# A two-layer decoder trunk in exact fp32: the MLA mask and maximum as one VectorE operation, values behind the scores of two groups, words for transposes, and small loads issued later

## The chip, the core and the metric

The kernel runs on one core of a Trainium2 chip. The metric is the time of one execution on the device in microseconds (us). The core has TensorE (PE: matrix products from SBUF into the accumulation memory PSUM; loading the stationary operand is shown apart as PEld), VectorE (DVE), ScalarE (ACT), GpSimd (POOL) and SyncE (SP, here the queue that issues the weight loads).

## The reference

Two residual layers over 256 positions of width 2048, all in float32. The even layer runs 32 state-space heads (convolution, silu, chunked scan) and 16 heads of latent attention (MLA) from one input projection, and projects both outputs together; the odd layer is stick-breaking attention; each is followed by a SwiGLU feed-forward part of 5632 hidden units.

```python
def reference(x, ...):
    for layer in range(2):
        h = rms_norm(x, mix_norm[layer])
        mix = ssd_mla_mixer(h, ...) if layer % 2 == 0 else stick_breaking_mixer(h, ...)
        x = x + mix
        x = x + swiglu_ffn(rms_norm(x, ffn_norm[layer]), w_gate[layer], w_up[layer], w_down[layer])
    return rms_norm(x, final_norm)

def mla_mixer(...):   # for each block of 128 query rows, queries q0 to q1
    s = (q_nope @ k_nope.T + q_pe @ k_pe.T) * 192 ** -0.5    # keys 0 to q1
    mask = jnp.arange(q1)[None, :] <= jnp.arange(q0, q1)[:, None]
    p = jax.nn.softmax(jnp.where(mask, s, -jnp.inf), axis=-1)
    out = p @ v
```

## The kernel before

**Exactness.** A weight tile of 128x2048 arrives as `w`. ScalarE casts it to fp32r (the form in which TensorE takes a 32-bit word in one pass) as the high part `wh` (line 346), and VectorE subtracts to get the low part in place of `w` (line 352). Activations are split in the same way. Each product of tiles is three matmuls: high by high, low by high, high by low (lines 460, 462 and 463 in `project`, 508 and 510 in `project_T`, and line 905 in `pair`, which does the large products by a scheme of seven block products M1 to M7, with sums and differences of weight tiles in `wsum` slots, line 852). A transpose is a matmul with an identity; `transpose` (lines 356 to 359) takes an fp32r source with the fp32r identity at line 357, and any other with the fp32 identity at line 359. A "twin" is a piece of SBUF that has two names: `raw` in fp32 and `words` in fp32r. The same holds for the residual blocks `xres` and `xwords`.

**Order.** TensorE's order is the order of the program. Small work runs as generator tasks: `spawn` starts one, each `yield n` puts it to sleep for n steps, and each `tick` (one step of a projection, mostly) wakes at most two tasks that are due. The other engines' orders come from a scheduler by priorities. Weight tiles have rising numbers `wprio`, tasks marked `URGENT` come ahead of them; the loads of weights are issued by SyncE in order of `wprio`.

**Start.** `constants` issues x and the first norm's gains on SyncE, and calls `small_loads` at once: ten loads on GpSimd's queue (four norms' gains, convolution weights and bias, the three head parameters `hp`, `rope`). `constant_tiles` makes the identities (`ident`, `ident_r`, and a bf16 `identb`), triangles and the bf16 mask tile `cmask`. The loaded rows are transposed on TensorE by `vectors` (line 314) at the end of the first input projection.

**Even layer.** `even` runs six projections for the convolution, two for the latent q and kv, four for the gate z, the output projection's state-space half, then the MLA groups and the output's MLA half. `conv` writes a block's channels into `s2` buffers and ends with a silu (line 1504); `ssd_group` transposes them (line 1562) four at a time.

**MLA.** `mla_group` handles four heads: it projects the rope half of q, then q, k and v, and spawns four `mla_head` tasks, four steps apart, which run during the next group's projections. A head makes scores in one PSUM tile of 128x384 (queries 0 to 127 against 128 keys, queries 128 to 255 against 256 keys): lines 1649 and 1650 multiply, and line 1651 adds the mask as a bf16 matmul of `identb` by `cmask`. VectorE takes two maxima (line 1656) and scales them (1657), ScalarE exponentiates with the sum (1659), VectorE divides. Seven steps later TensorE transposes p (line 1667, three transposes), ScalarE copies it (1669), and four steps later come the two products with v. Scores, transposes and products with v share a ring of four PSUM buffers, `tr`.

**Norms.** `norm_block` transposes a residual block of 512 columns in fours (through `transpose_split`). The blocks between the output projections and the feed-forward parts are spawned by `norm_next`; their blocks 2 and 3 read `xres`.

Of the kernel before, what the change touches and what calls it, by code (L numbers as in the profile page):

```python
# [15 lines left out]
P = 128  # L16
# [31 lines left out]
class Trunk:  # L48
# [84 lines left out]
    def weight_slots(self):  # L133
# [7 lines left out]
        for k in range(n):  # L141
# [27 lines left out]
        self.spare = [at(f"spare{q}", [P, 512], q) for q in range(8)]  # L169

    def wsum(self):
# [50 lines left out]
    def constants(self):  # L222
# [10 lines left out]
        for j in range(1, 4):  # L233
            with self.priority(self.wprio + 1000 * j - 500):
                nc.sync.dma_start(self.xres[j],
                                  i["x"][0, :, j * 512:(j + 1) * 512].rearrange("(t p) d -> p t d", p=P))
        with self.priority(self.wprio + 3500):
            self.small_loads(rows_a, rows_b)
        with self.priority(self.wprio + 6500):
# [11 lines left out]
    def small_loads(self, rows_a, rows_b):  # L251
        nc, i = self.nc, self.i
        c = lambda shape, name, dt=F32: self.cp.tile(shape, dt, name=name)
        for r0, r1, name in ((0, 32, "ffn_norm"), (32, 48, "ssd_norm"), (48, 52, "q_norm"), (52, 56, "kv_norm")):
            nc.gpsimd.dma_start(rows_a[r0:r1], i[name].rearrange("l (k p) -> (l k) p", p=P))
        nc.gpsimd.dma_start(rows_b[0:96], i["conv_w"].rearrange("e j (k p) -> (e j k) p", p=P))
        nc.gpsimd.dma_start(rows_b[96:120], i["conv_b"].rearrange("e (k p) -> (e k) p", p=P))
        self.hp = c([P, 3, 32], "hp")
        for r, name in enumerate(("dt_bias", "a_log", "d_skip")):
            nc.gpsimd.dma_start(self.hp[:, r, :], i[name][0:1, :].partition_broadcast(P))  # L260
        self.rope = c([P, 2, 2, 32], "rope")
        nc.gpsimd.dma_start(self.rope, i["rope"].rearrange("(t p) c d -> p t c d", p=P))


    def constant_tiles(self, rows_m, rows_a, rows_b):
# [24 lines left out]
        self.ones = self.ones_r.bitcast(F32)  # L290
        zero = self.s2([P])
        nc.gpsimd.memset(zero, 0.0)
# [997 lines left out]
    def even(self, st):  # L1290
        nc, i = self.nc, self.i
        win = i["w_in"][0]
        xT = self.pairs(st["xT"], True)
        xdt = [[self.spare[2 * n + t] for t in range(2)] for n in range(4)]
        y = [[self.s2([512]) for _ in range(2)] for _ in range(4)]
# [67 lines left out]
        oT = self.operand()  # L1363
        for g in range(4):
            self.mla_group(g, self.pairs(cT[:1]), self.pairs(cT[1:]), oT)
        st = self.norm_begin()
# [117 lines left out]
    def conv(self, n, res):  # L1484

        nc = self.nc
        for k2 in range(2):
            yield (8 if n == 4 else 2) if k2 == 0 else 1
            pt = self.tr([2, S])
            for k in range(2):  # L1490
                for t in range(2):
                    c = (2 * k2 + k) * P
                    self.transpose(pt[:, k, t * P:(t + 1) * P], self.twins[t].words[:, c:c + P])
            o = self.s2([2, S])
            res.append(o)
            for k in range(2):
# [33 lines left out]
    def ssd_group(self, g, conv, cconv, cb, xdt, y):  # L1530
# [28 lines left out]
        for t in range(2):  # L1559
            pt = self.tr([512])  # L1560
            for k in range(4):
                nc.tensor.transpose(pt[:, k * P:(k + 1) * P], xT[k // 2][:, k % 2, t * P:(t + 1) * P], self.ident)
# [23 lines left out]

    def mla_group(self, g, cq, ckv, oT):
# [3 lines left out]
        h0 = 4 * g  # L1591

        def heads(wd, c0, n):
            def view(w, k0, k1):
                for k in range(k0, k1):
                    yield (w[:, k - k0, :4 * n].rearrange("p (h c) -> p h c", c=n),
                           wd[:, k, h0:h0 + 4, c0:c0 + n])
            return view

        qp = self.evac_rope(self.project(cq, heads(wuq, 128, 64), 4, 256), self.twins[g % 2])  # L1600
        q = self.project_T(cq, heads(wuq, 0, 128))
        k = self.project_T(ckv, heads(wkv, 0, 128))
        v = self.evac(self.project(ckv, heads(wkv, 128, 128), 4))
        o, left = self.out_tiles(g), [0, 1, 2, 3]

        def done(h):
            left.remove(h)
            if g < 2 and not left:
                with self.priority(10000000):
                    self.operand_ready(oT, g, o, 1)  # L1610
        tasks = [self.spawn(self.mla_head(h, qp, q, k, v, g, o, 2 + 4 * h, done), self.URGENT) for h in range(4)]
        oT["xT"].append((self.spawn(self.wait_all(tasks)), o))

# [25 lines left out]
    def mla_head(self, h, qp, q, k, v, g, o, wait, done):  # L1639
# [7 lines left out]
        for q0, q1, c0, ks in ((0, P, 0, P), (P, S, P, S)):  # L1647
            dst = sc[:, c0:c0 + ks]
            nc.tensor.matmul(dst, qT[:, q0:q1], kT[:, 0:ks], start=True, stop=False)  # L1649
            nc.tensor.matmul(dst, qpT[:, q0:q1], self.kpeT[:, h % 2, 0:ks], start=False, stop=False)  # L1650
            nc.tensor.matmul(dst[:, ks - P:ks], self.identb, self.cmask, start=False, stop=True)
        mx, sm = self.small([P, 2], "mx"), self.small([P, 2], "sm")
        p = self.s2([3 * P])
        regs = (slice(0, P), slice(P, 3 * P))
        for t in range(2):
            nc.vector.tensor_reduce(mx[:, t:t + 1], sc[:, regs[t]], AX.X, ALU.max)
# [71 lines left out]
```

## Time and profile before

| | us |
|---|---|
| three runs | 2367.43, 2367.01, 2366.98 |
| median | 2367.01 |
| the profiled execution, its own time | 2367.28 |
| its span in the profile | 2365.2 |
| granted clock of TensorE, as a share | 0.998 |
| MLA heads on TensorE, start of the first scores to start of the last product with v | 422.6 to 553.8 |

The span is the time from the first to the last recorded instruction; 2.1 us lie around it. The profile's 40 slices have TensorE at nine tenths or more in all but the last. A row of a timeline tells the start, the duration, the engine, the line, the operation as output<-inputs, the sizes, the type and the number of joined records. TensorE's matmuls overlap, so that what one costs is read from the start of one to the start of the next. A row of the groups tells the total busy time, the mean in ns, and idle time just before with what ended it.

### The profile page before, as it was taken

To read this page: it belongs to the slowest core of one execution; us is meant where nothing else is said; L and a number is where in the kernel's file an instruction comes from. 1 tells how busy PE (TensorE), PEld (TensorE's weight loads), DVE (VectorE), ACT (ScalarE), POOL (GpSimd) and SP (SyncE) were. 2 spreads that over 40 slices of the span, in tenths; PEclk is the share of its full clock that TensorE was granted. 3 is DMA by queue.
4 is the path that set the end of the run, shared out by engine and by line. 5 is a ranking of instruction groups with operands and counts; after the bars stand their busy time and mean duration, and the time that the engine had idled before them with its cause. 6 is when DMAs were issued, how large, how long until landed. Compare 5 with 4: busy or idle time off the path is not lost.

```text
span 2365.2 us, 28220 instructions
## 1 busy us (share of the span) xinstructions
PE 2349.3 (99%) x11082; PEld 1953.9 (83%) x11082; DVE 2001.6 (85%) x1657; ACT 1467.2 (62%) x1486; POOL 215.7 (9%) x273
## 2 busy tenths in 40 slices
PE   9999999999999999999999999999999999999998
PEld 7888888988888888888888888888888888888886
DVE  6776587589998889989887898889997988989895
ACT  6655565566665655566665786776664656556664
POOL 1342001110000000000000020110000000000011
PEclk9999999999999999999999999999999999999999
DMA  7665556445666777777776555557667777767773
GB/s 273 204 194 179 184 196 188 135 142 195 231 203 207 225 217 215 223 219 221 218 241 207 203 182 176 185 175 242 226 203 213 216 228 221 217 214 228 216 253 110
DMA packets 271428, 486.33 MB, mean 206 GB/s; under 512 B 22268, under 2 KB 47488, under 8 KB 271296
## 3 DMA queue, kind: packets, MB, share of 16 engines
q1 hardware_dynamic: 255200, 445.95, 57.3%
q0 software_dynamic: 15232, 37.01, 6.5%
q8 instruction: 87, 1.43, 0.2%
q10 hardware_dynamic: 864, 1.57, 0.2%
q14 instruction: 45, 0.37, 0.0%
HBM read 459.24 MB, written 25.20 MB: 205 GB/s over the span
## 4 chain that ended last, share of the span: by engine, by line
PE 95%; DVE 2%; ACT 2%; issue 1%; DMA 0%; SPq 0%; ACTq 0%; DVEq 0%
PE acc L905 54%; PE acc L460 11%; PE acc L463 11%; PE acc L462 11%; PE tr L357 1%; PE acc L643 1%; PE acc L508 1%; ACT wh L346 1%; PE at L1578 1%; PE acc L510 0%; DVE wsum L852 0%; DVE wsum L352 0%; DVE w L352 0%; PE at L1649 0%; DMA xres<-in_x_dram 0%
## 5 line engine op out<-in xcount | busy, mean ns | idle before, releaser
L352 DVE TENSOR_TENSOR w<-w,wh 128x2048 fp32r<-128x2048 f32 (+2 forms) x399 | 893.4, 2246 | 174.8 <-ACT wh L346 168.4
L905 PE MATMUL acc<-wh,s 128*128 128x512 f32 x3896 | 985.4, 391 | 1.6 <-ACT s L926 1.2
L346 ACT CAST wh<-w 128x2048 fp32r<-128x2048 f32 (+2 forms) x399 | 744.5, 1874 | 322.9 <-PE acc L463 135.3
L905 PEld LDWEIGHTS acc<-wh,s 128*128 128x128 f32 x3896 | 725.5, 188 | 151.0 <-ACT s L926 1.7
L460 PE MATMUL acc<-wh,s 128*128 128x512 f32 (+1 forms) x1168 | 463.4, 397 | 0.1
L463 PE MATMUL acc<-wh,s 128*128 128x512 f32 (+1 forms) x1168 | 452.4, 387 | 0.2 <-DVE s L381 0.2
L462 PE MATMUL acc<-w,s 128*128 128x512 f32 (+1 forms) x1104 | 426.7, 387 | 0.0
L905 PE MATMUL acc<-w,s 128*128 128x512 f32 x1312 | 355.6, 389 | 0.2 <-DVE w L352 0.2
L905 PEld LDWEIGHTS acc<-w,s 128*128 128x128 f32 x1312 | 246.2, 188 | 52.1 <-DVE w L352 0.6
L463 PEld LDWEIGHTS acc<-wh,s 128*128 128x128 f32 x1168 | 219.3, 188 | 46.1 <-DVE s L381 0.6
L460 PEld LDWEIGHTS acc<-wh,s 128*128 128x128 f32 x1168 | 219.4, 188 | 43.6 <-issue 1.7
L462 PEld LDWEIGHTS acc<-w,s 128*128 128x128 f32 x1104 | 207.7, 188 | 40.0 <-issue 1.4
L352 DVE TENSOR_TENSOR wsum<-wsum,wh 128x2048 fp32r<-128x2048 f32 (+1 forms) x103 | 222.1, 2156 | 3.4 <-ACT wh L346 3.3
L346 ACT CAST wh<-wsum 128x2048 fp32r<-128x2048 f32 (+1 forms) x103 | 185.8, 1804 | 57.5 <-PE acc L905 38.4
L1067 POOL DMA_DIRECT2D saved<-s x64 | 55.9, 996 | 1107.0 <-ACT s L1066 1105.8
L346 ACT CAST wh<-lent 128x2048 fp32r<-128x2048 f32 (+1 forms) x62 | 114.6, 1858 | 62.4 <-DMA lent<-in_w_gate_dram 26.0
L352 DVE TENSOR_TENSOR lent<-lent,wh 128x2048 fp32r<-128x2048 f32 (+1 forms) x62 | 137.1, 2217 | 11.6 <-ACT wh L346 11.1
L852 DVE TENSOR_TENSOR wsum<-w,wsum 128x2048 f32<-128x2048 f32 (+1 forms) x54 | 106.7, 1976 | 19.2 <-PE acc L905 16.6
L905 PE MATMUL acc<-wsum,s 128*128 128x512 f32 x380 | 104.6, 390 | 1.4 <-DVE wsum L352 1.4
L905 PEld LDWEIGHTS acc<-wsum,s 128*128 128x128 f32 x380 | 71.2, 188 | 17.1 <-DVE wsum L352 2.2
L926 ACT COPY s<-acc 128x512 f32<-128x512 f32 x88 | 51.6, 588 | 39.1 <-PE acc L905 39.1
L852 DVE TENSOR_TENSOR wsum<-w,w 128x2048 f32<-128x2048 f32 (+1 forms) x36 | 72.6, 2017 | 1.7 <-DMA w<-in_w_qkv_dram 1.7
(280 smaller groups left out, 1966.8 us busy)
## 6 DMA issues: line engine op xcount, KB each, us to landing
w<-in_w_down_dram SPq DMA_DIRECT2D x80, 1024.0 KB, 4.9
w<-in_w_gate_dram SPq DMA_DIRECT2D x76, 1024.0 KB, 5.1
w<-in_w_up_dram SPq DMA_DIRECT2D x76, 1024.0 KB, 5.1
w<-in_w_qkv_dram SPq DMA_DIRECT2D x48, 1024.0 KB, 5.0
w<-in_w_in_dram SPq DMA_DIRECT2D x45, 1024.0 KB, 5.1
w<-in_w_out_even_dram SPq DMA_DIRECT2D x32, 1024.0 KB, 4.9
saved<-s POOLq DMA_DIRECT2D x64, 256.0 KB, 7.3
w<-in_w_out_odd_dram SPq DMA_DIRECT2D x16, 1024.0 KB, 5.0
```

The source lines that it names most:

```text
L346: cast = nc.scalar.copy(hi, src).ins
L352: return nc.vector.tensor_tensor(lo, src, hi.bitcast(F32), op=ALU.subtract).ins
L357: self.nc.tensor.transpose(out.bitcast(F32R), src, self.ident_r)
L460: nc.tensor.matmul(ps[t], hi[:, ts], wh, start=k == 0, stop=False)
L462: slot.used(nc.tensor.matmul(ps[t], hi[:, ts], wl, start=False, stop=False), self.clock)
L463: nc.tensor.matmul(ps[t], lo[:, ts], wh, start=False, stop=k == nk - 1)
L508: nc.tensor.matmul(ps[:, h % 2], wh[:, hs], x, start=k == n == 0, stop=False)
L643: m = nc.tensor.matmul(ps[b], x, y, start=b not in started, stop=stop, skip_group_check=True)
L852: ins = self.nc.vector.tensor_tensor(half(o, so), half(p, sp), half(q, sq), op=ALU.subtract).ins
L905: m = nc.tensor.matmul(ps[b], x, y, start=b not in started, stop=stop, skip_group_check=True)
L926: copied = nc.scalar.copy(o, ps[b]).ins
L1067: nc.gpsimd.dma_start(self.saved[n][:, t], s, accum_op=ALU.add)
```

## The change

Five edits stand in it.

**1. Mask and maximum.** The two mask matmuls of a head go, and with them `identb` and `cmask`. GpSimd fills a tile `mask` of 128x256 fp32 (zeros on the left, the causal mask on the right) behind the state-space half of the output projection. One VectorE operation a region adds the mask to the scores, multiplies by −scale, writes the result (the wide region in place in PSUM, the narrow one into p), and gives the minimum as the exponential's bias. The exponential's scale becomes −1.

**2. Values later.** `mla` takes the place of `mla_group`: scores of groups 0 and 1 first, then the values of both, then the same for 2 and 3. Heads of the second of a pair are three steps apart, and the first head of a pair waits eight steps, not four, before its products with v.

**3. Words.** Eight leases of 2 KB, each with an fp32 and an fp32r name, lie over the two `wsum` slots. The convolution's outputs for blocks 0 to 3 and p of eleven heads (groups 0 and 1, and three of group 2) stand there, and are transposed as words. So are blocks 2 and 3 of the norms behind the output projections; only the very first block keeps `xres`.

**4. Small loads.** `small_loads` runs as a task eight steps into the first projection, and each load waits for the latest weight cast on ScalarE at that point. On GpSimd the loads stand behind the triangles, `hp` and `rope` first.

**5. Filler.** A constant `more_filler` takes the room of what is gone, in the pool of constants.

```diff
@@ weight_slots
+        first = self.HIGH + self.LOW
+        lease = lambda k, name, dt: nc.alloc_sbuf_tensor_at(
+            f"{name}{k}", [P, 512], dt, offset=base + 8192 * first + 2048 * k).ap()
+        self.leases = [Twin(lease(k, "lease", F32), lease(k, "leasewords", F32R)) for k in range(8)]
...
@@ constants, small_loads, even
-        with self.priority(self.wprio + 3500):
+        def vectors_in():
+            yield 8
             self.small_loads(rows_a, rows_b)
+        def load(dst, src):
+            ins = nc.gpsimd.dma_start(dst, src).ins
+            self.tc.add_manual_dep(ins, self.cast.name, mybir.DependencyInfo(
+                mybir.DependencyClass.Sync, mybir.DependencyReason.DATA), reason="behind the first tiles")
+        self.spawn(self.vectors_in())
@@ constant_tiles
-        self.identb = c([P, P], "identb", BF16)
-        make_identity(nc, self.identb)
...
-        self.cmask = c([P, P], "cmask", BF16)
-        nc.gpsimd.affine_select(self.cmask, zero, [[-1, P]], ALU.is_ge, NEG, base=0, channel_multiplier=1)
+        c([P, P], "more_filler")
@@ norm_block
-        x = (self.xres if rank and rank < 100000 else self.xwords)[j]
+        x = (self.xres if rank == 99600 else self.xwords)[j]
@@ conv
-            o = self.s2([2, S])
-            res.append(o)
+            if n < 4:
+                o, w = (a.rearrange("p (k s) -> p k s", k=2) for a in self.lease(2 * n + k2))
+                res.append(w)
+            else:
+                o = self.s2([2, S])
+                res.append(o)
@@ ssd_group
-                nc.tensor.transpose(pt[:, k * P:(k + 1) * P], xT[k // 2][:, k % 2, t * P:(t + 1) * P], self.ident)
+                self.transpose(pt[:, k * P:(k + 1) * P], xT[k // 2][:, k % 2, t * P:(t + 1) * P])
@@ mla, in place of mla_group
+        for g in (0, 2):
+            scores(g, 4)
+            scores(g + 1, 3)
+            values(g)
+            values(g + 1)
@@ mla_head
-            nc.tensor.matmul(dst, qpT[:, q0:q1], self.kpeT[:, h % 2, 0:ks], start=False, stop=False)
-            nc.tensor.matmul(dst[:, ks - P:ks], self.identb, self.cmask, start=False, stop=True)
+            nc.tensor.matmul(dst, qpT[:, q0:q1], self.kpeT[:, h % 2, 0:ks], start=False, stop=True)
...
+        if g < 2 or g == 2 and h < 3:
+            p, words = (a[:, :3 * P] for a in self.lease(4 * (g > 0) + h))
+        else:
+            p = words = self.s2([3 * P])
...
-        for t in range(2):
-            nc.vector.tensor_reduce(mx[:, t:t + 1], sc[:, regs[t]], AX.X, ALU.max)
-        nc.vector.tensor_scalar(mx, mx, -scale, None, op0=ALU.mult)
-        for t in range(2):
-            nc.scalar.activation(p[:, regs[t]], sc[:, regs[t]], AF.Exp, scale=scale, bias=mx[:, t:t + 1],
+        for t in (1, 0):
+            with self.tc.issue_after(first) if first else nullcontext():
+                first = nc.vector.tensor_tensor_reduce((p, sc)[t][:, regs[t]], sc[:, regs[t]],
+                                                       self.mask[:, P * (1 - t):], -scale, -NEG, ALU.add, ALU.min,
+                                                       mx[t]).ins
+        for t in (1, 0):
+            nc.scalar.activation(p[:, regs[t]], (p, sc)[t][:, regs[t]], AF.Exp, scale=-1.0, bias=mx[t],
                                  accum_out=sm[:, t:t + 1])
...
-            nc.tensor.transpose(pt[:, b * P:(b + 1) * P], p[:, b * P:(b + 1) * P], self.ident)
+            self.transpose(pt[:, b * P:(b + 1) * P], words[:, b * P:(b + 1) * P])
...
-        yield 4
+        yield 8 if h == 0 and g % 2 == 0 else 4
```

TensorE at the first MLA head's scores, before; `at` is the PSUM tile of scores, `acc` that of the projection around it:

```order
L463 MATMUL acc_3280<-wh_67,s_201_1855 128x256
L1649 MATMUL at_3299<-s_303_3205,s_299_3145 128x128
L1650 MATMUL at_3299<-kpeT,s_306_3225 128x128
L1651 LDWEIGHTS identb
L1651 MATMUL at_3299<-cmask,identb 128x128
L1649 MATMUL at_3299<-s_303_3205,s_299_3145 128x256
L1650 MATMUL at_3299<-kpeT,s_306_3225 128x256
L1651 LDWEIGHTS identb
L1651 MATMUL at_3299<-cmask,identb 128x128
L460 MATMUL acc_3279<-wh_67,s_204_1881 128x256
```

The same place of the changed kernel, whose lines 1678 and 1679 are 1649 and 1650 of before:

```order
L474 MATMUL acc_3247<-wh_66,s_192_1853 128x256
L1678 MATMUL at_3266<-s_295_3208,s_291_3148 128x128
L1679 MATMUL at_3266<-kpeT,s_298_3228 128x128
L1678 MATMUL at_3266<-s_295_3208,s_291_3148 128x256
L1679 MATMUL at_3266<-kpeT,s_298_3228 128x256
L471 MATMUL acc_3246<-wh_66,s_195_1879 128x256
```

Two matmuls and their loads of the identity are gone, and the same projection matmul follows.

ScalarE at the end of the second convolution block, before; the two silus are L1504 ACTIVATE, and the casts are of weight tiles:

```order
L1499 ACTIVATE s_141_1178<-tr_1173,vb 128x256
L1553 ACTIVATE s_134_1138<-s_134_1138 128x512
L1504 ACT_TABLE_LOAD
L1504 ACTIVATE s_139_1157<-s_139_1157 128x512
L346 CAST wh_65<-w_76 128x2048
L1504 ACTIVATE s_141_1178<-s_141_1178 128x512
```

And of the changed kernel, where the silu is L1523, the cast L357, and the block stands in leases:

```order
L1518 ACTIVATE lease_112<-tr_1176,vb 128x256
L1572 ACTIVATE s_131_1142<-s_131_1142 128x512
L357 CAST wh_67<-w_74 128x2048
L1591 COPY s_138_1249<-at_1247 128x512
L1523 ACT_TABLE_LOAD
L1523 ACTIVATE lease_110<-lease_110 128x512
L1523 ACTIVATE lease_112<-lease_112 128x512
```

No cast stands between the two silus now; one cast and a copy that stood elsewhere come ahead of both.

VectorE at a head of group 1 in the changed kernel (L1689 is the new operation, which the program lists as two: the operation and the read of its minimum; L363 is a weight split):

```order
L1689 ISA at_3608,mx_357_3614<-at_3608,s_286_3065 128x256
L1689 ISA mx_357_3614 128x1
L363 TENSOR_TENSOR w_79<-w_80,wh_66 128x4x256
L1689 ISA lease_118,mx_356_3613<-at_3608,s_286_3065 128x128
L1689 ISA mx_356_3613 128x1
L1695 RECIPROCAL sm_3615<-sm_3615 128x2
L1697 TENSOR_SCALAR lease_118<-lease_118,sm_3615 128x128
L1697 TENSOR_SCALAR lease_118<-lease_118,sm_3615 128x256
```

A head of group 1 before, where L1656 is a maximum, L1657 the scaling of both, and L352 a weight split:

```order
L352 TENSOR_TENSOR w_79<-w_80,wh_66 128x2048
L1656 TENSOR_REDUCE mx_3618<-at_3611 128x1 x2
L1657 TENSOR_SCALAR mx_3618<-mx_3618 128x2
L352 TENSOR_TENSOR w_77<-w_78,wh_67 128x4x256
L1661 RECIPROCAL sm_3619<-sm_3619 128x2
L1663 TENSOR_SCALAR s_362_3620<-s_362_3620,sm_3619 128x128
L1663 TENSOR_SCALAR s_362_3620<-s_362_3620,sm_3619 128x256
```

The split, which stood behind the two maxima, stands between the two new operations.

More of the change, by code (lines that the diff above doesn't have):

```diff
@@ L169, in weight_slots, with lease @@
         self.spare = [at(f"spare{q}", [P, 512], q) for q in range(8)]
+    def lease(self, k):
+        return self.leases[k].raw, self.leases[k].words
     def wsum(self):
@@ L236, in constants @@
                                   i["x"][0, :, j * 512:(j + 1) * 512].rearrange("(t p) d -> p t d", p=P))
-        with self.priority(self.wprio + 3500):
+        def vectors_in():
+            yield 8
             self.small_loads(rows_a, rows_b)
+        self.vectors_in = vectors_in
         with self.priority(self.wprio + 6500):
@@ L252, in small_loads @@
         nc, i = self.nc, self.i
+        def load(dst, src):
+            ins = nc.gpsimd.dma_start(dst, src).ins
+            self.tc.add_manual_dep(ins, self.cast.name, mybir.DependencyInfo(
+                mybir.DependencyClass.Sync, mybir.DependencyReason.DATA), reason="behind the first tiles")
         c = lambda shape, name, dt=F32: self.cp.tile(shape, dt, name=name)
         for r0, r1, name in ((0, 32, "ffn_norm"), (32, 48, "ssd_norm"), (48, 52, "q_norm"), (52, 56, "kv_norm")):
-            nc.gpsimd.dma_start(rows_a[r0:r1], i[name].rearrange("l (k p) -> (l k) p", p=P))
-        nc.gpsimd.dma_start(rows_b[0:96], i["conv_w"].rearrange("e j (k p) -> (e j k) p", p=P))
-        nc.gpsimd.dma_start(rows_b[96:120], i["conv_b"].rearrange("e (k p) -> (e k) p", p=P))
+            load(rows_a[r0:r1], i[name].rearrange("l (k p) -> (l k) p", p=P))
+        load(rows_b[0:96], i["conv_w"].rearrange("e j (k p) -> (e j k) p", p=P))
+        load(rows_b[96:120], i["conv_b"].rearrange("e (k p) -> (e k) p", p=P))
         self.hp = c([P, 3, 32], "hp")
         for r, name in enumerate(("dt_bias", "a_log", "d_skip")):
-            nc.gpsimd.dma_start(self.hp[:, r, :], i[name][0:1, :].partition_broadcast(P))
+            load(self.hp[:, r, :], i[name][0:1, :].partition_broadcast(P))
         self.rope = c([P, 2, 2, 32], "rope")
-        nc.gpsimd.dma_start(self.rope, i["rope"].rearrange("(t p) c d -> p t c d", p=P))
+        load(self.rope, i["rope"].rearrange("(t p) c d -> p t c d", p=P))
     def constant_tiles(self, rows_m, rows_a, rows_b):
@@ L290, in constant_tiles @@
         self.ones = self.ones_r.bitcast(F32)
-        zero = self.s2([P])
-        nc.gpsimd.memset(zero, 0.0)
-        self.cmask = c([P, P], "cmask", BF16)
-        nc.gpsimd.affine_select(self.cmask, zero, [[-1, P]], ALU.is_ge, NEG, base=0, channel_multiplier=1)
+        c([P, P], "more_filler")
         self.vm, self.va, self.vb = c([P, 32], "vm"), c([P, 56], "va"), c([P, 120], "vb")
@@ L1363, in even @@
         oT = self.operand()
-        for g in range(4):
-            self.mla_group(g, self.pairs(cT[:1]), self.pairs(cT[1:]), oT)
+        self.mask = self.s2([2 * P])
+        nc.gpsimd.memset(self.mask, 0.0)
+        nc.gpsimd.affine_select(self.mask[:, P:], self.mask[:, P:], [[-1, P]], ALU.is_ge, NEG, base=0,
+                                channel_multiplier=1)
+        self.mla(self.pairs(cT[:1]), self.pairs(cT[1:]), oT)
         st = self.norm_begin()
@@ L1585, in ssd_group, with mla @@
         nc.gpsimd.tensor_tensor(y[1], y[1], yo, op=ALU.add)
-    def mla_group(self, g, cq, ckv, oT):
+    def mla(self, cq, ckv, oT):
         nc, i = self.nc, self.i
@@ L1590, in mla_group, with heads @@
         wkv = i["w_ukv"][0].rearrange("(k p) (h c) -> p k h c", p=P, c=256)
-        h0 = 4 * g
-        def heads(wd, c0, n):
+        def heads(wd, g, c0, n):
             def view(w, k0, k1):
@@ L1596, in view, with scores, done, values @@
                     yield (w[:, k - k0, :4 * n].rearrange("p (h c) -> p h c", c=n),
-                           wd[:, k, h0:h0 + 4, c0:c0 + n])
+                           wd[:, k, 4 * g:4 * g + 4, c0:c0 + n])
             return view
[L1600 to L1612, printed above, removed]
+        v = [[] for _ in range(4)]
+        def scores(g, gap):
+            qp = self.evac_rope(self.project(cq, heads(wuq, g, 128, 64), 4, 256), self.twins[g % 2])
+            q = self.project_T(cq, heads(wuq, g, 0, 128))
+            k = self.project_T(ckv, heads(wkv, g, 0, 128))
+            o, left = self.out_tiles(g), [0, 1, 2, 3]
+            def done(h):
+                left.remove(h)
+                if g < 2 and not left:
+                    with self.priority(10000000):
+                        self.operand_ready(oT, g, o, 1)
+            tasks = [self.spawn(self.mla_head(h, qp, q, k, v[g], g, o, 2 + gap * h, done), self.URGENT)
+                     for h in range(4)]
+            oT["xT"].append((self.spawn(self.wait_all(tasks)), o))
+        def values(g):
+            v[g] += self.evac(self.project(ckv, heads(wkv, g, 128, 128), 4))
+        for g in (0, 2):
[3 more added lines that the diff above has]
+            values(g + 1)
     def wait_all(self, tasks):
@@ L1649, in mla_head @@
             nc.tensor.matmul(dst, qT[:, q0:q1], kT[:, 0:ks], start=True, stop=False)
[L1650 to L1653, printed above, removed]
-        regs = (slice(0, P), slice(P, 3 * P))
-        for t in range(2):
-            nc.vector.tensor_reduce(mx[:, t:t + 1], sc[:, regs[t]], AX.X, ALU.max)
-        nc.vector.tensor_scalar(mx, mx, -scale, None, op0=ALU.mult)
-        for t in range(2):
-            nc.scalar.activation(p[:, regs[t]], sc[:, regs[t]], AF.Exp, scale=scale, bias=mx[:, t:t + 1],
+            nc.tensor.matmul(dst, qpT[:, q0:q1], self.kpeT[:, h % 2, 0:ks], start=False, stop=True)
+        mx, sm = [self.small([P, 1], f"mx{t}") for t in range(2)], self.small([P, 2], "sm")
+        if g < 2 or g == 2 and h < 3:
+            p, words = (a[:, :3 * P] for a in self.lease(4 * (g > 0) + h))
+        else:
+            p = words = self.s2([3 * P])
+        regs = (slice(0, P), slice(P, 3 * P))
+        first = None
+        for t in (1, 0):
[5 more added lines that the diff above has]
+            nc.scalar.activation(p[:, regs[t]], (p, sc)[t][:, regs[t]], AF.Exp, scale=-1.0, bias=mx[t],
                                  accum_out=sm[:, t:t + 1])
```

## Prediction

> **What bounds the kernel now.** I read the page's first part, then its chain of work, then TensorE's list of waits, because a kernel with one engine near 100% is changed only by what that engine does and by what it waits for.
>
> ```profile
> PE 2349.3 (99%) x11082; PEld 1953.9 (83%) x11082; DVE 2001.6 (85%) x1657; ACT 1467.2 (62%) x1486; POOL 215.7 (9%) x273
> ...
> PE 95%; DVE 2%; ACT 2%; issue 1%; DMA 0%; SPq 0%; ACTq 0%; DVEq 0%
> ```
>
> ```profile
> PE acc L905 <- DVE wsum L352: 1.4, 2, 0.7
> ...
> PE acc L905 <- ACT s L926: 1.2, 1, 1.2
> PE tr L357 <- DMA xres<-in_x_dram: 0.6, 1, 0.6
> PE at L1518 <- ACT s L1504: 0.6, 1, 0.6
> ```
>
> TensorE works for 2349.3 us of a span of 2365.2, and the chain is 95% TensorE. All its waits in the list together are under 8 us. So I count records that leave TensorE's sequence, records that get shorter, and waits that go or come. VectorE's 2001.6 us matter only in stretches where it is full. The sum is made against the profiled execution, 2367.28 us (its span and 2.1 us around it); the median of the three runs, 2367.01, lies 0.3 below it. About 0.2% of it, 4.7 us, is what a measurement of this kernel tells from no change, so "faster" means below 2362.3.
>
> **The mask leaves TensorE (32 matmuls).** Part of TensorE's own timeline around the first MLA head; the columns are start, duration, engine, line, operation and the number of records joined:
>
> ```profile
> 423.03 0.22 PE L1651 MATMUL at<-cmask,identb 128*128 128x128 bf16 x1
> 423.08 0.65 PE L1649 MATMUL at<-s,s 128*128 128x256 f32 x2
> 423.57 0.59 PE L1650 MATMUL at<-kpeT,s 128*128 128x256 f32 x2
> 424.00 0.22 PE L1651 MATMUL at<-cmask,identb 128*128 128x128 bf16 x1
> 424.03 0.36 PE L460 MATMUL acc<-wh,s 128*128 128x256 f32 x1
> 424.23 0.28 PE L462 MATMUL acc<-w,s 128*128 128x256 f32 x1
> 424.35 0.28 PE L463 MATMUL acc<-wh,s 128*128 128x256 f32 x1
> ```
>
> Durations overlap, so the cost is in the starts. The first mask starts at 423.03 and the next record at 423.08: 0.05 us. That next pair then takes 0.49 to its successor where the equal pair behind it takes 0.43: 0.06 more. The second mask takes 0.03, and the projection matmul behind it 0.20 (424.03 to 424.23) where the next takes 0.12: 0.08. Either way a mask costs 0.11 us, so 32 cost **3.5 us**. Bounds: the mask's own steps alone, 0.03 to 0.05, give 1.3; its recorded duration gives 7.0:
>
> ```profile
> L1651 PE MATMUL at<-cmask,identb 128*128 128x128 bf16 x32 | 7.0, 219 | 0.0
> ```
>
> I take 3.5, as the lengthened neighbours are measured.
>
> **Words for transposes.** Three kinds of transposes read fp32r instead of fp32: 32 of the state-space groups (L1562), 33 of the 48 at L1667, and 32 of the 40 at L359 (blocks 2 and 3 of the norms, in both layers). The two forms stand beside each other in the feed-forward part, each as four transposes followed by four matmuls of 128x512:
>
> ```profile
> 610.01 0.60 PE L359 MATMUL tr<-ident,xres 128*128 128x128 f32 x4
> 610.36 1.17 PE L905 MATMUL acc<-wh,s 128*128 128x512 f32 x4
> 611.38 0.60 PE L359 MATMUL tr<-ident,xres 128*128 128x128 f32 x4
> ```
>
> ```profile
> 664.93 0.46 PE L357 MATMUL tr<-ident_r,twinwords 128*128 128x128 f32 x4
> 665.23 1.16 PE L905 MATMUL acc<-wh,s 128*128 128x512 f32 x4
> 666.22 0.46 PE L357 MATMUL tr<-ident_r,twinwords 128*128 128x128 f32 x4
> ```
>
> From start to start the fp32 period is 1.37 us, the fp32r period 1.29: 0.08 for four transposes. The state-space groups are eight fours: **0.64**. The eleven heads have threes at 0.06: **0.66**. The norms would give another 0.64, but layer 0's stand in a stretch where TensorE is held up by VectorE anyway (below), and layer 1's before a second such wait, so I count **0.15**, with 0 and 0.64 as ends.
>
> **Small loads.** TensorE's start, the load queue's share of the first 12 us, and what the moved loads are needed for:
>
> ```profile
> 9.36 0.38 PE L309 MATMUL tr<-s 128*128 128x512 bf16 x1
> 10.39 0.50 PE L357 MATMUL tr<-ident_r,xwords 128*128 128x128 f32 x4 [0.64 <-DMA xres<-in_x_dram]
> ```
>
> ```profile
> q0 software_dynamic: 279, 0.19, 8.7%
> ...
> s<-in_ffn_norm_dram POOLq DMA_DIRECT2D x1, 16.0 KB, 5.8
> ```
>
> TensorE stands idle 0.64 us for a block of x. GpSimd's queue q0, with these ten loads, used 8.7% of 16 engines over 12 us, some 1.0 us of all of them, ahead of x and the first weight tiles. Without that x can come up to 1.0 us earlier and the wait goes: **0.6** (0 to 0.64; if x isn't what q0 delayed, nothing). The cover for the loads in their new place, in rows of ScalarE's, GpSimd's and TensorE's timelines:
>
> ```profile
> 13.99 1.07 ACT L346 CAST wh<-w 128x1024 fp32r<-128x1024 f32 x1
> 5.10 0.52 POOL L257 DMA_DIRECT2D s<-in_conv_b_dram  x1
> 33.30 0.52 PE L314 MATMUL tr<-ident,s 56*128 56x56 f32 x2
> ```
>
> They wait for the cast that ends at 15.06; ten issues of 0.52 us last to 20.3; with 5.8 us to land they are there at about 26, and the first reader, L314 on TensorE, comes at 33.30. On GpSimd nothing stands behind them before the rope products. Seven microseconds of cover: cost nothing.
>
> **The convolution blocks' silus.** The first two of the second block on ScalarE, and TensorE's records around the wait for the second:
>
> ```profile
> 133.04 0.63 ACT L1504 ACTIVATE s<-s 128x512 f32<-128x512 f32 x1
> 133.58 1.89 ACT L346 CAST wh<-w 128x2048 fp32r<-128x2048 f32 x1
> 135.38 0.62 ACT L1504 ACTIVATE s<-s 128x512 f32<-128x512 f32 x1
> ```
>
> ```profile
> 135.22 0.38 PE L1562 MATMUL tr<-ident,s 128*128 128x128 f32 x2
> 136.05 0.44 PE L1562 MATMUL tr<-ident,s 128*128 128x128 f32 x2 [0.45 <-ACT s L1504]
> ```
>
> A weight cast of 1.89 us stands between the two. In the changed order both silus stand side by side behind it, so the second ends about when it did or earlier by up to a cast, and the pair of transposes that took 0.83 (135.22 to 136.05) takes half of the 0.35 that four took above: **0.6** (0 to 0.65). The waits at L1518 and for L926 keep their neighbours; I count 0 for them (to 0.4 gained if the earlier heads free ScalarE before L926).
>
> **What is added.** Per head VectorE issues four instructions before the exponential instead of three: two in-place adds with a minimum, each with an accumulator read. No run shows that operation. Nearest rows, of VectorE from 400 to 560:
>
> ```profile
> L352 DVE TENSOR_TENSOR w<-w,wh 128x2048 fp32r<-128x2048 f32 x19 | 43.5, 2289 | 29.4 <-ACT wh L346 26.2 <-DMA w<-in_w_uq_dram 3.2
> ...
> L1656 DVE TENSOR_REDUCE mx<-at 128x1 f32<-128x256 f32 x16 | 6.6, 414 | 0.0
> ...
> L352 DVE TENSOR_TENSOR s<-at,s 128x256 fp32r<-128x256 f32 x8 | 3.4, 420 | 4.0 <-ACT s L346 4.0
> ```
>
> A reduction over 128x256 takes 0.414, an elementwise operation with two inputs, one from PSUM, 0.420. So the new one lies between 0.42 and both in a row, 0.83; I take 0.42, plus some 0.2 for its read. That is 0.3 to 1.2 us more per head, 5 to 19 us over sixteen heads, on an engine with idle time left:
>
> ```profile
> 500.00:550.00 50.00, 48.77 (x252) 40.98 (x251) 43.70 (x64) 34.69 (x61) 0.00 (x0) 1.00 0.41 136
> 550.00:600.00 50.00, 50.00 (x234) 41.55 (x233) 45.84 (x43) 29.73 (x33) 1.15 (x2) 1.00 0.63 212
> 600.00:650.00 50.00, 49.22 (x224) 40.10 (x223) 50.00 (x43) 35.78 (x38) 1.07 (x2) 1.00 0.70 237
> ```
>
> The third busy column is VectorE: 10.5 us idle between 500 and 600, none after 600. On TensorE the longer chain from scores to exponential must fit in the seven steps before the transposes. Values now come behind the scores of two groups, which adds work between scores and P·V for the first groups, but the value copies end shortly before the first P·V, the scores of group 1's last head take the PSUM buffer of its third head soon after that one's transposes, and a sum tile must wait for the last leased words. Each can turn into a wait like the smallest in the list, 0 to 0.6. I take **0.25** in all (the reorder itself could also gain up to that, as no matmul goes).
>
> **Sum.** 3.5 + 0.64 + 0.66 + 0.15 + 0.6 + 0.6 − 0.25 = 5.9; 2367.28 − 5.9 = 2361.4, put at **2361.5** for the rounding of 0.05 in the steps. The forecast's own range is 2359.6 (all upper ends of the small terms, 0.4 for L926, no new wait) to 2362.3 (start or silu giving nothing).
>
> **Rivals.**
> **1. VectorE takes the gain back.** Behind MLA it is full, and TensorE waits there:
>
> ```profile
> 625.81 0.73 PE L905 MATMUL acc<-wsum,s 128*128 128x512 f32 x2 [0.65 <-DVE wsum L352]
> ```
>
> If the added 5 to 19 us push the splits of the weight tiles up to that point, the MLA masks' and words' gain (3.5 + 0.66, less some that reaches the next layer) comes back as a longer wait at 625: 3 us, 2364.5. For it: 50.00 of 50. Against: 10.5 us idle shortly before, and splits whose releaser is a cast that itself waits for TensorE, so that an earlier TensorE makes them earlier too.
>
> **2. The masks cost only their own steps.** If the 0.06 and 0.08 behind a mask belong to the change of operand and stay, 32 times 0.04 is 1.3, and the gain 3.7: 2363.6. Against: the same surplus behind both masks, beside neighbours of the same kind without it. The Trainium skill ("TensorE: Matmul & The Clock Gate", section "Back-to-back issue gap") has 56 ns for an isolated matmul of 128 columns and about 81 ns in a stream with weight loads; 32 of these are 1.8 or 2.6 us. The trace's 0.11 is above both, and decides.
>
> **3. Slower: the reduction queues behind a split.** In the changed order a weight split can stand between a head's first and second reduction. Where it does and TensorE has come to that head's transposes, TensorE waits a whole split, 2.29. Two and a half such waits (5.9 / 2.29) cancel the gain; six of the sixteen heads give 13.7 and 2375.2. It decides if the seven steps of cover (each a projection step) don't hold 2.29 plus the reductions; no such wait exists now at L1667, which speaks against it. The Trainium skill ("VectorE: DVE Perf Modes", section "Rules for kernel authors") says of chained operations: "Don't try to fuse for perf — DRAIN happens regardless. Minimize op *count*, not sems". By that rule three instructions becoming four is a loss on VectorE; the rows give 0.3 us a head at the lower end, in agreement, but off the path while the cover holds.
>
> **Chances.** Forecast 0.60; rival 1 0.17; rival 2 0.08; rival 3 with one to three waits (2362.5 to 2368) 0.08, with more 0.07. Faster 0.60, same 0.33, slower 0.07. The range runs from 2359.6 to 2365.0, past rivals 1 and 2; outside are rival 3's upper part and a gain above all the ends.
>
> **What would show it.** Right: no L1651 in TensorE's groups and 32 mask steps gone; fours of transposes at L357's 0.46 where 0.60 stood; no wait for x near 10 and none at 136; TensorE's busy time down by some 4.5 us and its waits by 1 to 1.5. Wrong: a longer wait for a sum tile near 620 (rival 1), a pair of score matmuls as long as now without a mask (rival 2), waits of TensorE at the heads' transposes or P·V on VectorE or ScalarE (rival 3), or a wait at L314 for the late loads.

## The result, and the profile after

| kernel | median us | runs | ratio to before, 95% interval |
|---|---|---|---|
| before | 2367.22 | 4 | |
| changed | 2423.89 | 4 | 1.024 (1.0227 to 1.0252) |

The change makes the kernel 56.7 us slower. Two views of the changed kernel answer to those shown first in the prediction, the busy times and the chain of work that ended last:

```profile
PE 2399.3 (99%) x11050; PEld 1953.2 (81%) x11050; DVE 2006.3 (83%) x1673; ACT 1469.8 (61%) x1486; POOL 221.8 (9%) x271
...
PE 90%; issue 6%; POOL 1%; DVE 1%; ACT 1%; POOLq 0%; ACTq 0%
```

TensorE has the 32 matmuls less that were to go (11082 to 11050), and 50.0 us more of busy time (2349.3 to 2399.3). Its weight loads are as long as before, VectorE and ScalarE differ by under 5 us. And 6% of the chain is "issue", where the profile shows nothing waited for; it was 1%, and the runs below show that this is no sign of what slows the kernel. Then TensorE's waits:

```profile
PE tr L368 <- POOL twin L1497: 6.1, 1, 6.1
PE acc L519 <- ACT s L1654: 2.4, 1, 2.4
PE acc L916 <- DVE wsum L363: 1.5, 2, 0.8
...
PE acc L916 <- ACT s L937: 0.7, 1, 0.7
```

The waits for x at the start and for the silu at L1562 are gone, that for the block product's copies (L937, before L926) is 0.7 in place of 1.2. Two new ones stand in MLA, 8.5 us together. That leaves some 48 us, and all that was gained besides, which no wait explains. They lie in every large matmul. The group of the commonest form, before and then after (busy time, mean ns):

```profile
L905 PE MATMUL acc<-wh,s 128*128 128x512 f32 x3896 | 985.4, 391 | 1.6 <-ACT s L926 1.2
```

```profile
L916 PE MATMUL acc<-wh,s 128*128 128x512 f32 x3896 | 1008.7, 397 | 0.7 <-ACT s L937 0.7
```

The same in TensorE's timeline, in a projection of the second layer far from every edit; before:

```profile
999.81 0.39 PE L462 MATMUL acc<-w,s 128*128 128x512 f32 x1
...
1000.94 0.39 PE L460 MATMUL acc<-wh,s 128*128 128x512 f32 x1
```

and after:

```profile
1024.25 0.39 PE L474 MATMUL acc<-wh,s 128*128 128x512 f32 x1
...
1026.34 0.40 PE L474 MATMUL acc<-wh,s 128*128 128x512 f32 x1
```

Five steps take 1.13 us before, 0.226 each; nine take 2.09 after, 0.232 each. About 9,400 matmuls have this form (5844 in the block products, three times 1136 in the projections, 138 elsewhere), so 6 ns each are some 56 us. The granted clock doesn't explain it: it is 0.997 after and 0.998 before.

One thing differs for all of these matmuls, and the profile doesn't show it: the address of their stationary operand. In the memory map of the two programs the pool of activations (`s2`) starts at byte 147200 of each partition before, and at 147264 after. `identb` and `cmask` (512 bytes) are replaced by `more_filler` (512 bytes), but the small tile `mx` of two columns, with two buffers of 32 bytes, became two tiles with two such buffers each: 64 bytes more ahead of the pool. 147200 is a multiple of 256; 147264 is not.

### The profile page after: what moved, and what is told of

Read it like the earlier page. It is cut to its first block, busy times and chain, and to the rows that moved or that the text cites. A ratio compares the mean times of both kernels' runs of the same rounds, so it can differ in the third digit from the quotient of the medians.

```text
span 2421.8 us, 28168 instructions
## 1 busy us (share of the span) xinstructions
PE 2399.3 (99%) x11050; PEld 1953.2 (81%) x11050; DVE 2006.3 (83%) x1673; ACT 1469.8 (61%) x1486; POOL 221.8 (9%) x271
## 3 DMA queue, kind: packets, MB, share of 16 engines
q8 instruction: 87, 1.43, 0.2%
## 4 chain that ended last, share of the span: by engine, by line
PE 90%; issue 6%; POOL 1%; DVE 1%; ACT 1%; POOLq 0%; ACTq 0%
PE acc L916 52%; PE acc L471 11%; PE acc L474 11%; PE acc L473 11%; PE tr L368 1%; PE acc L654 1%; PE at L1597 1%; POOL ropea L1491 0%; POOL twin L1497 0%; PE at L1216 0%; PE at L1261 0%; POOL ropeb L1492 0%; PE at L1292 0%; DVE s L392 0%; DVE wsum L363 0%
## 5 line engine op out<-in xcount | busy, mean ns | idle before, releaser
L363 DVE TENSOR_TENSOR w<-w,wh 128x2048 fp32r<-128x2048 f32 (+2 forms) x399 | 894.0, 2248 | 193.5 <-ACT wh L357 187.8
L916 PE MATMUL acc<-wh,s 128*128 128x512 f32 x3896 | 1008.7, 397 | 0.7 <-ACT s L937 0.7
L357 ACT CAST wh<-w 128x2048 fp32r<-128x2048 f32 (+2 forms) x399 | 744.1, 1873 | 349.0 <-PE acc L474 150.3
L471 PE MATMUL acc<-wh,s 128*128 128x512 f32 (+1 forms) x1168 | 470.0, 402 | 0.1
L474 PE MATMUL acc<-wh,s 128*128 128x512 f32 (+1 forms) x1168 | 458.3, 392 | 0.2 <-DVE s L392 0.2
L473 PE MATMUL acc<-w,s 128*128 128x512 f32 (+1 forms) x1104 | 432.7, 392 | 0.0
L916 PE MATMUL acc<-w,s 128*128 128x512 f32 x1312 | 363.9, 396 | 0.1
L473 PEld LDWEIGHTS acc<-w,s 128*128 128x128 f32 x1104 | 207.8, 188 | 45.5 <-issue 1.7
L357 ACT CAST wh<-wsum 128x2048 fp32r<-128x2048 f32 (+1 forms) x103 | 185.7, 1803 | 66.6 <-PE acc L916 34.1
L363 DVE TENSOR_TENSOR wsum<-wsum,wh 128x2048 fp32r<-128x2048 f32 (+1 forms) x103 | 222.2, 2157 | 4.6 <-ACT wh L357 4.6
L357 ACT CAST wh<-lent 128x2048 fp32r<-128x2048 f32 (+1 forms) x62 | 114.5, 1857 | 63.8 <-DMA lent<-in_w_gate_dram 25.0
L363 DVE TENSOR_TENSOR lent<-lent,wh 128x2048 fp32r<-128x2048 f32 (+1 forms) x62 | 137.2, 2218 | 13.1 <-ACT wh L357 12.8
L937 ACT COPY s<-acc 128x512 f32<-128x512 f32 x88 | 51.7, 587 | 46.7 <-PE acc L916 46.5
```

Of the source, the lines that this page charges most:

```text
L357: cast = nc.scalar.copy(hi, src).ins
L363: return nc.vector.tensor_tensor(lo, src, hi.bitcast(F32), op=ALU.subtract).ins
L471: nc.tensor.matmul(ps[t], hi[:, ts], wh, start=k == 0, stop=False)
L473: slot.used(nc.tensor.matmul(ps[t], hi[:, ts], wl, start=False, stop=False), self.clock)
L474: nc.tensor.matmul(ps[t], lo[:, ts], wh, start=False, stop=k == nk - 1)
L916: m = nc.tensor.matmul(ps[b], x, y, start=b not in started, stop=stop, skip_group_check=True)
```

## The experiments

All times are medians, beside runs of the kernel before on the same chip in the same batch (2367.0 to 2367.4 in each).

**Placement.** Four kernels move the activations' pool. The first is the changed kernel with a smaller filler, which moves the small tiles between filler and pool too:

```diff
-        c([P, P], "more_filler")
+        c([P, 112], "more_filler")
```

> The changed kernel with its unused constant more_filler cut from 512 to 448 bytes, so that the activation buffers start at address 147200 again, as before the change, and not 64 bytes higher. Theory (placement): TensorE's 128x512 matmuls, whose stationary operands are activations, fall from 233 ns apart back to 227, which is worth some 54 us; the two waits in MLA (2.4 and 6.1 us) stay: about 2370 us. Rival (some other part of the change slows TensorE everywhere, for instance the leases or the new VectorE operation): 233 ns stays, 2424 us.

Measured 2372.11, ratio 1.0021 (1.0012 to 1.0031). So 51.8 of the 56.7 us go with 64 bytes. The other three leave the kernel before as it is, move nothing but the pool, and put an unused tile of 64, 32 and 128 bytes ahead of the pool (16, 8 or 32 columns):

```diff
+        ec(tc.tile_pool(name="pad", bufs=1)).tile([P, 16], F32, name="pad")
         self.ap = ec(tc.tile_pool(name="acts", bufs=40))
```

> The kernel before, with nothing but 64 unused bytes ahead of the activation buffers (147264 in place of 147200). Placement: 227 becomes 233 ns at every 128x512 matmul, about 2420 us. Rival (no effect of placement): 2367 us.

> The kernel before with 32 unused bytes ahead of the activation buffers (147232). Placement with a grain of 64 bytes or more: as slow as with 64 bytes or slower, 2420 us or more. Placement with a grain of 32: 2367 us.

> The kernel before with 128 unused bytes ahead of the activation buffers (147328, a multiple of 128 but not of 256). Placement with a grain of 128 bytes: 227 ns and 2367 us; with a grain of 256: slower, up to 2420 us.

Measured 2420.77, 2419.44 and 2414.47: 47 to 54 us slower, without any other edit. The chain and two groups of TensorE in the kernel with 64 bytes; the first group of before stands above, its chain in the prediction:

```profile
PE 96%; DVE 2%; ACT 1%; DMA 0%; issue 0%; SPq 0%; ACTq 0%; DVEq 0%
...
L906 PE MATMUL acc<-wh,s 128*128 128x512 f32 x3896 | 1008.8, 397 | 1.4 <-ACT s L927 1.4
...
L509 PE MATMUL acc<-s,wh 128*128 128x256 f32 x256 | 36.4, 284 | 0.0
```

The first group has the changed kernel's mean to the nanosecond. The second is `project_T`, where the weights are stationary and the activations move: 284 against 287 before, so of the two operands it is the stationary one whose address costs. The chain has no "issue", though this kernel is slow by the address alone, while e1_align, and e_outp below, with the pool at 147200, have 6% like the changed kernel. That share comes from the wait for GpSimd in MLA: the chain is followed back from it along GpSimd's queue, through stretches in which GpSimd had nothing to do. A fifth takes x_both (below) and moves the pool down by 256 bytes, with a filler of 48 columns:

> x_both with the activation buffers 256 bytes lower (146944, again a multiple of 256). If TensorE's spacing goes by multiples of 256 bytes: 227 ns and 2362 us as x_both. If 147200 is good for another reason (its distance from the weight tiles, or a larger grain): 229 ns or more between matmuls, 2380 to 2415 us.

Measured 2362.23, against x_both's 2362.15. Two multiples of 256 are fast, and offsets of 32, 64 and 128 from one are slow; that fits a grain of 256 bytes, though other places were not tried.

**The two waits in MLA.** With placement mended, 7.1 us of waits are left in e1_align, and more behind them. Three rows of ScalarE's timeline there (L1693 is the exponential, L1654 the copy of group 3's rope part of q out of PSUM):

```profile
477.01 1.91 ACT L357 CAST wh<-w 128x2048 fp32r<-128x2048 f32 x1 [2.16 <-issue]
...
484.59 0.47 ACT L1693 ACTIVATE lease<-at,mx 128x256 f32<-128x256 f32 x1 [4.83 <-DVE mx L1689]
...
485.95 0.64 ACT L1654 COPY s<-acc 128x256 f32<-128x256 f32 x2
```

VectorE in the same stretch (the new operation is CUSTOM at L1689, its read stands behind it):

```profile
479.12 2.29 DVE L363 TENSOR_TENSOR w<-w,wh 128x2048 fp32r<-128x2048 f32 x1
481.32 0.43 DVE L1689 CUSTOM_DVE_ANT_0 at<-at,s 128x256 f32<-128x256 f32 x1
...
482.00 2.29 DVE L863 TENSOR_TENSOR wsum<-w,w 128x2048 f32<-128x2048 f32 x1 [0.17 <-DMA w<-in_w_out_even_dram]
484.21 0.28 DVE L1689 CUSTOM_DVE_ANT_0 lease<-at,s 128x128 f32<-128x128 f32 x1
```

GpSimd's first and last instruction of group 3's rope, and TensorE's records that waited:

```profile
486.40 0.84 POOL L1491 TENSOR_TENSOR ropea<-s,rope 128x128 f32<-128x128 f32 x1 [22.16 <-ACT s L1654]
...
497.51 0.98 POOL L1497 TENSOR_TENSOR twin<-ropea,ropeb 128x128 f32<-128x128 f32 x1
```

```profile
486.37 2.08 PE L519 MATMUL acc<-s,wh 128*128 128x256 f32 x8 [2.38 <-ACT s L1654]
...
498.55 0.75 PE L368 MATMUL tr<-ident_r,twinwords 128*128 128x128 f32 x4 [4.72 <-POOL twin L1497]
499.10 2.04 PE L519 MATMUL acc<-s,wh 128*128 128x256 f32 x8
```

The chain reads: a weight split, the wide reduction, a sum of weight tiles, the narrow reduction on VectorE; the exponential behind it on ScalarE, then the rope copy, 9 us after its projection had ended (476.9); the rope on GpSimd, 12 us long; and TensorE, which needs it. The eight matmuls from 499.10 take 0.23 each (to 500.93, the next start), where eight before the wait take 0.12: TensorE runs at half speed for about four microseconds behind the wait. Windows of e1_align behind each of the two waits show the granted clock, the third figure from the right (0.50):

```profile
486.30:489.10 2.80, 2.73 (x12) 2.73 (x13) 2.27 (x5) 2.80 (x8) 2.70 (x4) 0.50 0.78 301
...
498.50:502.00 3.50, 3.45 (x17) 3.46 (x18) 1.23 (x2) 0.00 (x0) 0.00 (x0) 0.50 0.00 0
```

Two causes were at hand: a VectorE instruction between a head's two reductions, or the new order of values. Four kernels, all with the pool at 147200, tell them apart. In e_outp the wide reduction writes into p as well, so that the second one depends on nothing of the first and follows at once in every head's program order (in e1_align, something stands between in six of sixteen):

```diff
-                first = nc.vector.tensor_tensor_reduce((p, sc)[t][:, regs[t]], sc[:, regs[t]],
+                first = nc.vector.tensor_tensor_reduce(p[:, regs[t]], sc[:, regs[t]],
...
-            nc.scalar.activation(p[:, regs[t]], (p, sc)[t][:, regs[t]], AF.Exp, scale=-1.0, bias=mx[t],
+            nc.scalar.activation(p[:, regs[t]], p[:, regs[t]], AF.Exp, scale=-1.0, bias=mx[t],
```

> The aligned kernel (e1_align) whose wide reduction also writes into p, not in place in PSUM. Its second reduction then depends on nothing of the first, and the program's order has no other VectorE instruction between the two reductions of any head; in e1_align there is one in 6 of 16 heads. Theory (a split between the reductions holds the exponentials, they hold the copies behind them on ScalarE, and TensorE waits twice in MLA): the waits of 2.4 and 4.7 us and the slow matmuls behind each go, about 11 us, 2361 us. Rival (the reorder leaves the rope too few steps): the 4.7 stay, 2369 to 2372 us.

In x_order the values follow their own group's scores again (heads start while these values are projected, four steps earlier than before the change), and the reductions stay in place; x_mask keeps the new order and takes back the mask matmuls, the two maxima and the scaling; x_both is e_outp with the order of x_order:

```diff
-        for g in (0, 2):
-            scores(g, 4)
-            scores(g + 1, 3)
-            values(g)
-            values(g + 1)
+        for g in range(4):
+            scores(g, 4)
+            values(g)
...
-        yield 8 if h == 0 and g % 2 == 0 else 4
+        yield 4
```

> e1_align with the values of each group again behind its own scores, heads four steps apart and four steps before P.V; the reductions stay as in the change, in place. Theory (split between the reductions): some splits stay, so a wait of 2 us or more stays somewhere in MLA, 2363 to 2370 us. Rival (reorder): both waits go, 2361 us.

> e1_align with the mask again as two bf16 matmuls and the maximum as two reductions and a scaling, in the changed order of values. Theory (split between the reductions): no wait in MLA, 2361 us plus the masks' 3.5 us, 2364.5. Rival (reorder): the waits stay and the masks come on top, about 2375 us.

> e_outp with the values again behind each group's own scores: alignment, words, loads and the VectorE mask, without the reorder. If the reorder is worth nothing by itself: the same as e_outp within 1 us, 2361. If the reorder gives TensorE cover that the longer chain of the new operation needs: slower by a wait at P.V, 2362 to 2365 us.

| values | reductions | kernel | us | ratio (interval) |
|---|---|---|---|---|
| behind two groups | in place | e1_align | 2372.11 | 1.0021 (1.0012 to 1.0031) |
| behind two groups | both into p | e_outp | 2366.62 | 0.9999 (0.9990 to 1.0008) |
| behind two groups | as before, with mask matmuls | x_mask | 2373.45 | 1.0028 (1.0018 to 1.0039) |
| behind own group | in place | x_order | 2363.65 | 0.9984 (0.9975 to 0.9993) |
| behind own group | both into p | x_both | 2362.15 | 0.9980 (0.9971 to 0.9988) |

Neither cause alone was right. x_mask has no new operation and still waits 1.9 and 3.8 us at the same two places, so the order is enough. The order here is the whole of the change's second edit, the place of the values, the three steps between heads and the eight before P·V; these were not tried one by one. e_outp loses the first wait and keeps 3.4 of the second, so the gap between the reductions adds to it. In the old order the gap costs 1.5 (2363.65 to 2362.15), in the new one 5.5 (2372.11 to 2366.62). These prices are rough. x_order's ten times fall into two groups: four are at 2362.1 to 2362.3, as in x_both, among them the profiled one, which has no wait in MLA; six are at 2363.65 to 2365.14, and no trace shows what they wait for. e_outp's eleven times spread over 3.8 us.

x_rope asks whether it is the late copy: e_outp, with the rope's copies marked urgent.

```diff
         for t in range(2):
-            nc.scalar.copy(qp[:, t], ps[t])
+            with self.urgent():
+                nc.scalar.copy(qp[:, t], ps[t])
```

> e_outp (alignment, both reductions into p, the changed order of values) with the two copies of a group's rope part marked urgent on ScalarE: for group 3 they then stand behind one head's exponentials and ahead of the next weight cast, where they stood behind two heads' exponentials and that cast. Theory (the late copy makes GpSimd's rope late, and TensorE waits 3.4 us for it and then runs slow for some 2 us): the copy comes within 3 us of its projection, the wait goes, about 2361 us. Rival (the changed order is slow for another reason, such as GpSimd's rope itself): the wait stays above 2 us, 2365 to 2367 us.

Measured 2363.72, ratio 0.9986 (0.9977 to 0.9995). Its waits:

```profile
PE at L1680 <- DVE s L1665: 1.8, 1, 1.8
...
PE tr L368 <- POOL twin L1497: 0.5, 1, 0.5
```

The copy comes 1.8 us behind its projection, and 2.9 of the 3.4 us go. But a step later TensorE now waits 1.8 for VectorE to copy the transposed rope. The late copy was the cause; VectorE's queue is the next limit. In x_both, without the reorder, GpSimd's last product of this rope ends 1.5 us ahead of TensorE's transposes (496.07 and 497.53), and VectorE's copy isn't waited for.

**What the rest is worth.** x_nomask is x_both with the mask as before the change: alignment, words, later loads and heads ahead of values are left.

> Alignment, words and later loads alone: the mask as bf16 matmuls, the maximum as reductions, and the values behind each group's scores, all as before the change. Prediction's terms without the mask: 0.64 + 0.66 + 0.15 + 0.6 + 0.6 = 2.65 us below before, 2364.4; against x_both (2362.15) the mask operation would then be worth 2.2 us, where the prediction has 3.5, so 2365.6 if the 3.5 is right.

Measured 2364.76, ratio 0.9990 (0.9981 to 0.9999). The terms without the mask sum to 2.65 and measure 2.4, with an interval from 0.2 to 4.5. The mask operation is then worth 2.6 in x_both. The waits of the two profiled executions differ in both directions: L937 waits 1.6 in x_both against 0.7, and the start 0.5 against 1.4. So the mask's own price is better read from TensorE's steps. The scores of a head with the same projection matmuls behind it, the first before and then the second in x_both (L1676 is L1649, L473 is L462):

```profile
422.58 0.39 PE L1649 MATMUL at<-s,s 128*128 128x128 f32 x2
...
424.23 0.28 PE L462 MATMUL acc<-w,s 128*128 128x256 f32 x1
```

```profile
422.43 0.39 PE L1676 MATMUL at<-s,s 128*128 128x128 f32 x2
...
423.86 0.28 PE L473 MATMUL acc<-w,s 128*128 128x256 f32 x1
```

From the first score matmul to the second projection matmul behind them it is 1.65 before and 1.43 in x_both: 0.22 a head, and 0.21 to 0.22 where other matmuls stand behind a head. That is 3.5 over sixteen, the term of the prediction.

Last, the prediction's sum by itself: e_outp with values projected ahead of their heads, so that TensorE's order is that of before, less the 32 masks.

```diff
             k = self.project_T(ckv, heads(wkv, g, 0, 128))
+            values(g)
             o, left = self.out_tiles(g), [0, 1, 2, 3]
...
-        for g in (0, 2):
-            scores(g, 4)
-            scores(g + 1, 3)
-            values(g)
-            values(g + 1)
+        for g in range(4):
+            scores(g, 4)
...
-        yield 8 if h == 0 and g % 2 == 0 else 4
+        yield 4
```

> e_outp with TensorE's order exactly that of before the change, less the 32 mask matmuls, and with words in the transposes: each group's values are projected ahead of its heads again. This is the prediction's sum without placement, without the reorder and without a split between the reductions. If its terms are right: 2361.5 us, with no wait in MLA but the one for the first block product's copies. If the longer chain on VectorE and the rope's small slack (0.6 us before the change) cost something in the old order too: a wait at the rope's transposes or at P.V, 2362.5 to 2364 us.

Measured 2369.32, ratio 1.0009 (1.0000 to 1.0018): neither. MLA's heads have no wait, but the first block product of the output projection has one, with slow matmuls behind it; TensorE, then VectorE ahead of it:

```profile
519.16 1.65 PE L916 MATMUL acc<-wh,s 128*128 128x512 f32 x3 [4.84 <-DVE s L363]
```

```profile
507.42 2.28 DVE L863 TENSOR_TENSOR wsum<-w,wsum 128x2048 f32<-128x2048 f32 x1
509.62 2.29 DVE L363 TENSOR_TENSOR wsum<-wsum,wh 128x2048 fp32r<-128x2048 f32 x1
...
516.22 2.28 DVE L363 TENSOR_TENSOR wsum<-wsum,wh 128x2048 fp32r<-128x2048 f32 x1
518.43 0.68 DVE L363 TENSOR_TENSOR s<-s,s 128x512 fp32r<-128x512 f32 x1
```

Five weight operations stand ahead of a split of 0.68 us that TensorE needs. Before the change it stood ahead of them. The priorities are the same in both; the scheduler picks by them among what it takes to be ready at a moment, and why the moment moved wasn't tried. With heads four steps earlier (x_both) the sums are done in time.

## Why the prediction was wrong

- **The step that failed** is one that isn't there. The sum counts "records that leave TensorE's sequence, records that get shorter, and waits that go or come"; it has no term for where the untouched operands come to lie. The exchange of constants and of `mx` was given no cost, and it is 51.8 us of the 56.7. The profile of before could not have shown it, since its large matmuls all had the good address; the allocation of the two programs, compared, would have shown the 64 bytes, but not their price.
- **"I take 0.25 in all"** for new waits in MLA is the term mis-sized: e1_align less x_both is 10.0 us. Of this 7.1 are waits, and the rest is about what the half-speed matmuls behind both lose (1.4 behind 486.37, 1.8 behind 499.10, each the stretch less its usual steps). Rival 3 had one part of it, a split of 2.29 between the reductions, but looked at the wrong reader: not the head's own transposes, which had their seven steps, but another group's rope copy behind the exponential on ScalarE. The other part is the reorder, which is enough for both waits without any new reduction (x_mask); the prediction had it in the 0.25.

What should have been read is the slack of that rope in the profile of before. GpSimd's last instruction of group 3 and TensorE's reader:

```profile
498.25 0.79 POOL L1482 TENSOR_TENSOR twin<-ropea,ropeb 128x128 f32<-128x128 f32 x1
```

```profile
499.65 0.46 PE L357 MATMUL tr<-ident_r,twinwords 128*128 128x128 f32 x4
```

The rope was done at 499.04, 0.6 us ahead. The prediction listed slacks at P·V, the PSUM ring and a sum tile, and not this one.

- **Words, loads and silus**: 2.65 forecast, 2.4 measured, with the interval above. The wait at L1562 went. The one at L926 fell from 1.2 to 0.7 in the changed kernel and in x_nomask, but rose to 1.6 in x_both. The start's 0.6 isn't shown: of ten profiled executions with the later loads, three have no wait there (the changed kernel, x_order, x_exact), and seven wait 0.5 to 1.4 us for x or for the first norm's gains.
- **The mask**: 3.5 forecast and 3.5 by TensorE's steps; 2.6 between the whole kernels. The new operation took 0.429 for 128x256 and 0.11 for its read, so the 0.42 taken for it, from the split with one input in PSUM, was right, and the 0.2 for the read too much. Rival 2, masks that cost only their own steps, is ruled out by the 0.22 a head; x_both's gain of 4.9, with an interval from 2.8 to 6.9, would not rule out its 3.7.
- **Rival 1**, VectorE behind MLA taking the gain back, didn't come: the wait for sum tiles is 1.8 in x_both and 1.4 before.
- **The range's lower end**, 2359.6, is not what its terms give: the upper ends named sum to 7.1, or 7.4 if the reorder gains 0.25, which is 2360.2 or 2359.9 from 2367.28.
- With address, gap and reorder undone, x_both is at 2362.15, ratio 0.9980, faster than both kernels, and 0.65 from the 2361.5 of the forecast. x_exact shows that this is no proof of the sum: its terms hold only while VectorE's order leaves them their cover.

## What to carry to other kernels

Compare the memory map, not only the instructions: a small tile more can move every operand behind it, and on a kernel bound by matmuls the address of the stationary operand was worth 2%. Where matmuls grow by the same few nanoseconds everywhere, at the same granted clock, look there first; "issue" in the chain, which ran along an idle queue here, told nothing of it. When work is moved, read the slack of each transfer between engines that spans the move, those of other groups included, and price a wait with the slow matmuls behind it.

## What the runs showed of the hardware

- A stationary operand of 128x128 fp32r words that starts 32, 64 or 128 bytes past a multiple of 256 makes a 128x512 matmul 5 to 6 ns longer (mean 391 before, 397, 397 and 396 with 32, 64 and 128 bytes); a moving operand of 128x256 so placed cost nothing (287 to 284 with 64 bytes).
- Behind some idle stretches TensorE ran at half speed: 0.23 in place of 0.12 per 128x256 matmul after idle times of 2.38 and 4.72 us (e1_align), but not after 2.35 (changed kernel, 0.13 a matmul from 492.35) or 3.42 (e_outp). The Trainium skill ("TensorE: Matmul & The Clock Gate", section "What's actually happening") tells of a free-running window of about 3.4 us, behind which an idle array is clocked at half. A window with a phase of its own would fit that nearly equal idle times end differently here, but 2.38 us is shorter than one such window.
- GpSimd's rope products of 128x128 took 0.45 to 0.98 each, and 2.4 to 2.5 us in single cases (490.28 in e1_align) while VectorE was at work on weight tiles; what makes the difference wasn't tried.
